# Even attention of a hybrid DiT step: value products in one run per head, score tiles spread a head ahead, TensorE in program order

## The chip, the cores and the metric

The kernel runs on one core of a Trainium2 chip. The time is that of one execution on the device, in microseconds (us). TensorE is called PE in the profile, its weight loads PEld, VectorE is DVE, ScalarE is ACT, GpSimd is POOL and SyncE, which issues the transfers here, is SP.

## The reference

One inference step of a two-layer backbone, for 128 prompt tokens and 512 sample tokens of width 1024. The even layer, on which the change bears, has 8 heads of latent attention (MLA) and 8 query heads on 2 key heads (GQA) side by side; the odd layer (mLSTM and differential attention) is left as it is.

```python
def attend(q, k, v):
    ...
        s = jnp.einsum('bqhgd,bthd->bhgqt', qi, k).astype(jnp.float32) * scale
        p = jax.nn.softmax(s, axis=-1).astype(v.dtype)
        return jnp.einsum('bhgqt,bthd->bqhgd', p, v)
...
    o_a = attend(q_a, k_a, v_a).reshape(B, S, MLA_W) * jax.nn.silu(g_a)
    ...
    o_b = attend(q_bg, kb_all, vb_all).reshape(B, S, GQA_W) * jax.nn.silu(g_b)
    return jnp.concatenate([o_a, o_b], axis=-1) @ w_out, new
```

Each layer is `x + gate * mix(rmsnorm(x) * (1 + scale) + shift)`, where `shift`, `scale` and `gate` are products of a conditioning vector with a weight ("adaptive norm"). Sample queries see 128 cached and 512 own keys, 640 in all; prompt queries see the prompt's 128 keys.

## The kernel before

The even attention (`attention`, L675 to L712, called by `even_attention`, L808 to L833) goes through 16 heads, MLA first. For each head the 512 sample queries are four tiles of 128.

- A **score tile** (`scores`, L596) is 128 queries by 640 keys in two halves of 320: three passes for MLA (the third is the low part `ql` of the queries), two for GQA, into one of two PSUM buffers (`s2`). VectorE takes the negated maximum `nm` (L603), ScalarE the exponential `p` with its sum (L606), VectorE the reciprocal `rs` (L609), GpSimd the normalisation (L616).
- A **transpose group** (`head_T`, L623) turns key tile k of all four query tiles into one PSUM buffer of two (`t1`); ScalarE copies it to `pT` (L628), VectorE for k = 2 (L626).
- The **value products** (`head_PV`, L634) of key tile k are two matmuls side by side, each on 64 columns of the array (`tile_position` (0, 0) and (0, 64)), and add into `o`. With five key tiles a head has ten of these instructions; the trace counts each as two rows. At the head's end `o` is multiplied into the gate buffer `og` (L710).
- `prompt_quad` (L638 to L673) does the prompt's attention for four heads in four stages: queries, scores `sp`, transposes `t1p`, products `op`.
- `side(h)` puts other work into a head: in heads 0 to 7 the odd layer's adaptive columns (`ada_cols`: L177, sixteen rows of 32 columns, a copy `adap` L180, two transposes L184, a reduction and three small VectorE additions, L190 to L195), in heads 8 to 15 the even layer's gate parts (`ada_gate_part`: L210, also 32 columns, copy `gp` L212), the loads of the output projection's weights (`op_load`: `raw`, three buffers shared with the gate's weights; `whi` on ScalarE, L76, `wlo` on GpSimd, L77) and the split of the first half of `og` into `oh` (ScalarE, L841) and `ol` (VectorE, L842). `ada_gate_row` sums the gate's parts (`gsum`, L221), which later go out and come back as a broadcast for the residual.

In the code, key tile k's products are written right after the transposes of key tile k + 1, and score tiles of later heads are written in between by a running count. The code order is only a priority: a scheduler that follows dependences and engine availability sets the order on every engine, TensorE included, and so the order of the sixteen heads' pieces is interleaved. Work on ScalarE, VectorE and GpSimd runs one instruction after another in the order in which it was issued.

Of the kernel before, what the change touches and what calls it, by code (L numbers as in the profile page):

```python
# [37 lines left out]
class K:  # L38
# [3 lines left out]
    # ---------------------------------------------------------------- helpers  # L42
# [8 lines left out]
    def sumsq(self, src, n, w):  # L51
        """sum of squares over groups of w: src [128, n*w] in SBUF -> [128, n]"""
# [14 lines left out]
    def wload(self, src, n, w, pool=None, pre="w", bufs=2, cp=None):  # L67
        """stream a [128, n, w] weight tile and split it into two float32r parts"""
# [18 lines left out]
    def lin_tok(self, pieces, ncols, hh, hl, toks, evac, pool, tag="acc", bufs=5):  # L87
        """out[token, col] for token tiles toks; pieces: [(dram ap, nk)]"""
# [12 lines left out]
    def drain(self, toks, evac, lag=3):  # L101
        """evacuate psum; what evac returns is done lag tiles later"""
# [9 lines left out]
    def lin_feat(self, src, hh, hl, pool, tag="acc", bufs=5):  # L112
        """out[col (128), token (640)] in two psum tiles of 320 tokens"""
# [9 lines left out]
    def silu_from(self, out, src, shape, pool, other=None):  # L123
        """out = silu(src) (times other); src may be PSUM"""
# [8 lines left out]
    def rope(self, out, x, cos, sin, nh, w, pool, rep=1, dup=False):  # L133
        """out = rope(x), [128, nh, w] views; cos, sin [128, w / rep]"""
# [26 lines left out]
    # ---------------------------------------------------------------- adaLN  # L161
# [8 lines left out]
    def ada_cols(self, L, kk, pool, tag, bufs, raws=None, split=False):  # L170
        """shift and gain of feature tile kk as [128, 2] columns (sample, prompt)"""
# [10 lines left out]
        def rest():  # L182
            for i in range(2):
                nc.tensor.transpose(ps[:, 256 + 128 * i:384 + 128 * i], part[:, i * 128:i * 128 + 128], self.ident)  # L184
            red = self.st.tile([128, 2, 2], F32, tag="adar", name="adar", bufs=2)
            nc.vector.tensor_reduce(out=red, in_=ps[:, 256:512].rearrange("p (i g j) -> p i j g", i=2, g=4)[:, :, 0:2],
                                    axis=AX.X, op=ALU.add)
            vg, vs, vc = (V_EG, V_EBS, V_EBC) if L == "e" else (V_OG, V_OBS, V_OBC)
# [11 lines left out]

    def ada_gate_part(self, L, kk, pool, tag, bufs):
        """partial rows of the gate of feature tile kk"""
# [11 lines left out]
    def ada_gate_row(self, L, pool, tag, bufs):  # L214
        """sum of the partial rows of the gate, to DRAM"""
# [12 lines left out]
    def ada_gate_bc(self, L, to):  # L228
        """gate broadcast over partitions: [128, 2, 1024], sample and prompt"""
        self.gate = to  # L230
        for c in range(2):
            self.nc.sync.dma_start(to[:, c], self.gd[L][c:c + 1].to_broadcast([128, 1024]))

    # ---------------------------------------------------------------- body
    def run(self):
        tc, nc, A = self.tc, self.nc, self.A
        with ExitStack() as es:
# [12 lines left out]
            self.GS = {L: (main.tile([128, 8, 2], F32, name="G" + L), main.tile([128, 8, 2], F32, name="S" + L))  # L250
                       for L in "eo"}
# [27 lines left out]
    # ---------------------------------------------------------------- even layer  # L279
    def even(self):  # L280
# [15 lines left out]
        head[0](0, P)  # L296
        head[0](1, P)
# [1339 lines left out]
```

## Time and profile before

| | |
|---|---|
| time, median of 3 runs | 914.14 us (911.05 to 916.01) |
| span of the profiled execution | 905.8 us |
| median less span | 8.3 us |
| TensorE busy | 852.9 us, 94% of the span |
| VectorE, ScalarE, GpSimd busy | 541.2, 422.6, 396.6 us |
| even attention, first score tile to first product of the output projection | 223.0 to 402.1 us |

The profile has no separate time of the profiled execution beside its span; the span counts from its first instruction to its last, and the three timed runs lie 5.3 to 10.2 us above it. Start times are from the start of the span. The busy time of TensorE is modelled from pipelined records, so what one row costs is best read as the step from its start to the next row's start.

### The profile page before, as it was taken

The page shows a single profiled execution, that of the slowest core. Times are in us where ns is not written, and L with a number is a line of the kernel's source. Part 1 is how long each engine was busy: PE and PEld are TensorE (multiplying, and loading weights), DVE is VectorE, ACT ScalarE, POOL GpSimd, SP SyncE. Part 2 cuts the span into 40 slices and gives each one's busy share as a digit, 9 for nine tenths or more (in the row PEclk, how much of TensorE's full clock was granted, in tenths as well). Part 3 has the DMA queues.
Part 4 walks back from the last instruction along what each step waited for, and adds up shares of the span by engine and source line. Part 5 has one row for each costly group of instructions (what it writes and reads, how often), then busy time and mean ns, then how long its engine had stood idle before and what let it go on. Part 6 is the DMA issues. An engine that isn't in the chain of part 4 may idle for free.

```text
span 905.8 us, 14374 instructions
## 1 busy us (share of the span) xinstructions
PE 852.9 (94%) x5418; PEld 707.2 (78%) x5418; DVE 541.2 (60%) x1125; ACT 422.6 (47%) x928; POOL 396.6 (44%) x302
## 2 busy tenths in 40 slices
PE   6999899979999999999999999999999899999997
PEld 2778788879776766668887889889989688778786
DVE  3773831993866877641386735077774736666765
ACT  5354523311655677752263324266554656443422
POOL 0144424751754646725535333422221946354930
PEclk9999999999999999999999999999999999999999
DMA  9821222220221222324412212222123122142503
GB/s 347 330 65 35 88 87 71 70 71 24 94 94 53 84 98 93 119 77 176 152 47 105 86 71 94 81 70 71 47 93 129 58 88 63 55 164 75 163 1 117
DMA packets 29641, 88.52 MB, mean 98 GB/s; under 512 B 3752, under 2 KB 6880, under 8 KB 29572
## 3 DMA queue, kind: packets, MB, share of 16 engines
q1 hardware_dynamic: 25904, 83.64, 26.4%
q10 hardware_dynamic: 3668, 3.96, 1.3%
q8 instruction: 43, 0.70, 0.3%
q14 instruction: 26, 0.21, 0.1%
HBM read 80.90 MB, written 6.68 MB: 97 GB/s over the span
## 4 chain that ended last, share of the span: by engine, by line
PE 74%; DVE 16%; issue 3%; ACT 3%; POOL 2%; DMA 1%; SPq 0%; POOLq 0%; ACTq 0%; DVEq 0%
PE acc L84 11%; PE acc L85 11%; PE acc L83 11%; PE s L596 7%; PE acc L1060 6%; PE o L634 5%; PE t L623 5%; PE acc L120 3%; PE o L1146 2%; PE pv L1460 2%; PE ada L177 1%; POOL wlo L77 1%; DVE nm L603 1%; PE gps L210 1%; PE acc L544 1%
## 5 line engine op out<-in xcount | busy, mean ns | idle before, releaser
L77 POOL TENSOR_TENSOR wlo<-raw,whi 128x1024 fp32r<-128x1024 f32 (+4 forms) x79 | 185.8, 2357 | 229.8 <-ACT whi L76 222.7
L85 PE MATMUL acc<-whi,Hl 128*128 128x512 f32 (+2 forms) x400 | 148.5, 373 | 1.6 <-DVE Hl L958 1.6
L84 PE MATMUL acc<-wlo,Hh 128*128 128x512 f32 (+2 forms) x400 | 149.2, 373 | 0.2 <-POOL wlo L77 0.2
L83 PE MATMUL acc<-whi,Hh 128*128 128x512 f32 (+2 forms) x400 | 138.9, 374 | 1.0 <-ACT qk L1064 1.0
L76 ACT CAST whi<-raw 128x1024 fp32r<-128x1024 f32 (+4 forms) x71 | 71.6, 1010 | 131.2 <-PE acc L85 80.5
L603 DVE TENSOR_REDUCE nm<-s 128x1 f32<-128x640 f32 (+1 forms) x104 | 80.9, 780 | 57.1 <-PE s L596 56.0
L616 POOL TENSOR_TENSOR p<-p,rs 128x640 f32<-128x640 f32 x64 | 79.7, 1256 | 64.2 <-DVE rs L609 62.6
L606 ACT ACTIVATE p<-s,nm 128x640 f32<-128x640 f32 (+1 forms) x104 | 79.4, 764 | 59.8 <-DVE nm L603 53.9
L85 PEld LDWEIGHTS acc<-whi,Hl 128*128 128x128 f32 x400 | 75.3, 188 | 14.7 <-DVE Hl L958 1.8
L83 PEld LDWEIGHTS acc<-whi,Hh 128*128 128x128 f32 x400 | 75.1, 188 | 14.0 <-ACT qk L1064 1.2
L84 PEld LDWEIGHTS acc<-wlo,Hh 128*128 128x128 f32 x400 | 75.4, 188 | 12.9 <-POOL wlo L77 0.6
L48 POOL TENSOR_TENSOR rs_r<-rs_h,mhalf 128x1 f32<-128x1 f32 (+4 forms) x39 | 35.6, 921 | 53.4 <-DVE rs_h L47 45.0
L623 PEld LDWEIGHTS t<-cst,p 128*128 128x128 f32 x320 | 34.6, 140 | 23.6 <-issue 22.1
L623 PE MATMUL t<-cst,p 128*128 128x128 f32 x320 | 51.3, 283 | 0.2 <-POOL p L616 0.2
L84 PE MATMUL acc<-wlo,oh 128*128 128x512 f32 (+1 forms) x124 | 48.1, 388 | 0.1
L85 PE MATMUL acc<-whi,ol 128*128 128x512 f32 (+1 forms) x124 | 47.8, 386 | 0.0
L83 PE MATMUL acc<-whi,oh 128*128 128x512 f32 (+1 forms) x124 | 46.7, 389 | 0.0
L628 ACT COPY pT<-t 128x512 f32<-128x512 f32 x64 | 37.1, 584 | 17.4 <-PE t L623 17.0
L120 PE MATMUL acc<-Hh,whi 128*128 128x320 f32 x128 | 31.3, 316 | 6.9 <-DVE og L129 6.9
L63 DVE TENSOR_REDUCE ssq<-sq 128x2 f32<-128x128 f32 (+3 forms) x19 | 11.5, 604 | 40.6 <-ACT sq L61 40.4
L885 ACT ACTIVATE junk<-xt 128x512 bf16<-128x512 f32 (+1 forms) x21 | 12.8, 610 | 49.0 <-DVE xt L883 37.7
L1060 PE MATMUL acc<-Hh,whi 128*128 128x320 f32 x128 | 32.5, 323 | 0.5 <-ACT v L1037 0.5
(380 smaller groups left out, 1983.2 us busy)
## 6 DMA issues: line engine op xcount, KB each, us to landing
adaw<-in_eada_ss_dram SPq DMA_DIRECT2D x16, 512.0 KB, 10.3
raw<-in_oada_ss_dram SPq DMA_DIRECT2D x16, 512.0 KB, 4.3
raw<-in_e_wG_dram SPq DMA_DIRECT2D x8, 512.0 KB, 3.3
raw<-in_eada_g_dram SPq DMA_DIRECT2D x8, 512.0 KB
raw<-in_e_wO_dram SPq DMA_DIRECT2D x8, 512.0 KB, 4.2
raw<-in_oada_g_dram SPq DMA_DIRECT2D x8, 512.0 KB, 3.5
raw<-in_o_wO_dram SPq DMA_DIRECT2D x8, 512.0 KB, 3.9
xT<-in_xT_dram SPq DMA_DIRECT2D x8, 320.0 KB, 5.8
```

What stands on the lines that cost most here:

```text
L76: (cp or nc.scalar.copy)(hi[:, 0:m], raw[:, 0:m])
L77: nc.gpsimd.tensor_tensor(out=lo[:, 0:m], in0=raw[:, 0:m], in1=hi[:, 0:m], op=ALU.subtract)
L83: mm(out, lhsT=lh, rhs=rh, start=first, stop=False)
L84: mm(out, lhsT=lh, rhs=rl, start=False, stop=False)
L85: self.mark = mm(out, lhsT=ll, rhs=rh, start=False, stop=last)
L120: mm(acc[j][:, 0:320], lhsT=a[:, k], rhs=b[:, k, j * 320:j * 320 + 320], start=f, stop=l)
L596: self.mark = self.nc.tensor.matmul(out[:, j, 0:w], lhsT=q[0:rows, qcols], rhs=k[0:rows, a:a + w], start=i == 0, stop=i == len(passes) - 1)
L603: nc.vector.tensor_reduce(out=nm, in_=s, axis=AX.XY, op=ALU.max, negate=True)
L606: nc.scalar.activation(out=p[:, 0:n].rearrange("p (a b) -> p a b", a=s.shape[1]), in_=s, func=AF.Exp, bias=nm, accum_out=sm)
L616: self.nc.gpsimd.tensor_tensor(out=p, in0=p, in1=rs.to_broadcast([128, 640]), op=ALU.mult)
L623: self.nc.tensor.transpose(tp[:, i * 128:i * 128 + 128], p[i][:, k * 128:k * 128 + 128], self.ident)
L1060: nc.tensor.matmul(acc[j][:, 0:320], lhsT=a[:, k], rhs=b[:, k, j * 320:j * 320 + 320], start=f, stop=l)
```

## The change

1. The ten value products of a head are written after its fifth transpose group, in one run; `o` is allocated there. The `pT` buffers go from 3 to 7, the `p` buffers from 10 to 8.
2. Score tiles are written one after each transpose group: tiles 1, 2 and 3 of the next head after groups 0, 1 and 2, and tile 0 of the head after that behind group 4. Prompt stages go behind group 3, or 4 for the last stage.
3. A context `pe_order` ties each TensorE instruction of the attention to the one before it in the code, so that TensorE runs in the order in which the program is written. It adds no semaphore wait. The other engines stay with the scheduler.
4. `side(h)` comes behind the products: one feature tile of adaptive columns per head 0 to 7, whose two transposes and reduction come a score tile later in the next head; the additions of shift and gain are done once for all eight tiles (`ada_close`). One gate part per head 8 to 15; the gate's sum follows the last products.
5. `prep` is split in `keys` (the cast and low part `Ka` of a head's keys) and `queries` (transposes and split), each at its own place.
6. The split of the first half of `og` takes its low part on GpSimd; that of the second half stays on VectorE.

```diff
+    @contextmanager
+    def pe_order(self):
...
+        for a, b in zip(pe, pe[1:]):
+            self.tc.add_manual_dep(b, a.name, mybir.DependencyInfo(mybir.DependencyClass.NoSync,
+                                                                   mybir.DependencyReason.DATA), reason="pe_order")
...
-        p, rs = self.softexp(T, s, 640, 10)
+        p, rs = self.softexp(T, s, 640, 8)
...
-        pT = T.tile([128, 512], F32, tag='pT', name='pT', bufs=3)
+        pT = T.tile([128, 512], F32, tag='pT', name='pT', bufs=7)
...
         for h in range(nh):
-            o = ps.tile([128, 512], F32, tag='o', name='o', bufs=1)
-            pt = {}
             p = [tiles.pop((h, i)) for i in range(4)]
-            for k in range(6):
-                if k < 5:
-                    pt[k] = self.head_T(T, ps, p, k)
-                if k:
-                    self.head_PV(o, V[h], cols[h], pt.pop(k - 1), k - 1)
-                if k == 0 and h + 2 < nh:
-                    prep(h + 2, P)
-                if k == 2:
-                    side(h)
-                if k in (3, 5):
-                    next(stages, None)
-                more_scores(4 * h + 5 + 1 + min(k, 3) + (1 if k >= 4 else 0))
+            pt = [self.head_T(T, ps, p, 0)]
+            if h + 2 < nh:
+                prep[0](h + 2, P)
+            scores(h + 1, 1)
+            if rest:
+                rest()
+            pt.append(self.head_T(T, ps, p, 1))
+            scores(h + 1, 2)
+            if h + 2 < nh:
+                prep[1](h + 2, P)
+            pt.append(self.head_T(T, ps, p, 2))
+            scores(h + 1, 3)
+            pt.append(self.head_T(T, ps, p, 3))
+            done = stage(0, 1, 2)
+            pt.append(self.head_T(T, ps, p, 4))
+            scores(h + 2, 0)
+            if not done:
+                stage(3)
+            o = ps.tile([128, 512], F32, tag='o', name='o', bufs=1)
+            for k in range(5):
+                self.head_PV(o, V[h], cols[h], pt[k], k)
...
+            rest = side(h)
...
-                for i in ((0, 1), (2,), (3,), (4,), (5,), (), (6,), (7,))[h]:
-                    self.ada_cols('o', i, ps, 'pr', 1)
+                rest = self.ada_cols('o', h, ps, 'pr', 1, split=True)
+                return rest if h < 7 else lambda: (rest(), self.ada_close())
...
-            for i in ((0,), (1,), (2,), (3,), (), (4,), (5, 6), (7,))[h - 8]:
-                self.ada_gate_part('e', i, ps, 'pr', 1)
+            self.ada_gate_part('e', h - 8, ps, 'pr', 1)
...
-        self.nc.vector.tensor_tensor(out=lo, in0=src, in1=hi, op=ALU.subtract)
+        (self.nc.vector if m else self.nc.gpsimd).tensor_tensor(out=lo, in0=src, in1=hi, op=ALU.subtract)
```

TensorE in an MLA head, before; `t` are transpose groups, `o` value products (one row of x2 is one key tile), `s` score tiles, `ada` the transposes of adaptive columns, `qtp` queries:

```order
L634 MATMUL o<-pT,Va 64x256 x2
L184 MATMUL ada<-cst,adap 128x128 x2
L634 MATMUL o<-pT,Va 64x256 x2
L623 MATMUL t_2550<-cst,p 128x128 x4
L634 MATMUL o<-pT,Va 64x256 x2
L623 MATMUL t_2587<-cst,p 128x128 x4
L777 MATMUL qtp<-cst,qa 128x128 x4
L634 MATMUL o<-pT,Va 64x256 x2
L623 MATMUL t_2639<-cst,p 128x128 x4
L634 MATMUL o<-pT,Va 64x256 x2
L623 MATMUL t_2657<-cst,p 128x128 x4
```

The same engine in an MLA head after the change, from the third transpose group on:

```order
L621 MATMUL s_3061<-Ka_1592,qh 128x320 x2
L621 MATMUL s_3061<-Ka_1591,ql 128x320 x2
L648 MATMUL t_3076<-cst,p 128x128 x4
L685 MATMUL t1p<-cst,pp 128x128 x4
L648 MATMUL t_3090<-cst,p 128x128 x4
L621 MATMUL s_3097<-Ka_1593,qh 128x320 x2
L621 MATMUL s_3097<-Ka_1594,qh 128x320 x2
L621 MATMUL s_3097<-Ka_1593,ql 128x320 x2
L659 MATMUL o<-pT,Va 64x256 x10
L190 MATMUL ada<-raw,sc 32x256 x8
L648 MATMUL t_3140<-cst,p 128x128 x4
```

The products stand in one run of ten behind the fifth group and a score tile, with the 32-column products of the adaptive norm right behind them.

GpSimd around the move from MLA to GQA heads, before; `p` are normalisations of score tiles, `pp` those of the prompt, `wlo` the low part of a piece of output weights:

```order
L656 TENSOR_TENSOR pp<-pp,sm_2953 128x512
L616 TENSOR_TENSOR p<-p,rs 128x640 x7
L656 TENSOR_TENSOR pp<-pp,sm_3254 128x512
L616 TENSOR_TENSOR p<-p,rs 128x640 x11
L77 TENSOR_TENSOR wlo<-raw,whi 128x1024
L616 TENSOR_TENSOR p<-p,rs 128x640 x7
L77 TENSOR_TENSOR wlo<-raw,whi 128x1024
```

And after:

```order
L641 TENSOR_TENSOR p<-p,rs 128x640 x13
L884 TENSOR_TENSOR ol_3679<-og,oh_3678 128x512
L884 TENSOR_TENSOR ol_3812<-og,oh_3811 128x512
L884 TENSOR_TENSOR ol_3936<-og,oh_3935 128x512
L884 TENSOR_TENSOR ol_4088<-og,oh_4087 128x512
L884 TENSOR_TENSOR ol_4217<-og,oh_4216 128x512
L641 TENSOR_TENSOR p<-p,rs 128x640 x3
L681 TENSOR_TENSOR pp<-pp,sm_3503 128x512
L641 TENSOR_TENSOR p<-p,rs 128x640 x10
L77 TENSOR_TENSOR wlo<-raw,whi 128x1024
```

The five low parts of the split stand in one row among the normalisations; before, they were on VectorE.

ScalarE in a GQA head in which output weights are loaded, before:

```order
L606 ACTIVATE p,sm<-s_3848,nm 128x640
L628 COPY pT<-t_3801 128x512
L76 CAST whi<-raw 128x1024
L212 COPY gp<-gps 128x128
L606 ACTIVATE p,sm<-s_3870,nm 128x640
L606 ACTIVATE p,sm<-s_3892,nm 128x640
L628 COPY pT<-t_3861 128x512
L628 COPY pT<-t_3883 128x512
```

And after:

```order
L653 COPY pT<-t_3815 128x512
L653 COPY pT<-t_3835 128x512
L631 ACTIVATE p,sm<-s_3822,nm 128x640
L76 CAST whi<-raw 128x1024
L631 ACTIVATE p,sm<-s_3842,nm 128x640
L653 COPY pT<-t_3875 128x512
L844 CAST qp<-qtp 64x2x128
L631 ACTIVATE p,sm<-s_3862,nm 128x640
L653 COPY pT<-t_3890 128x512
L631 ACTIVATE p,sm<-s_3897,nm 128x640
```

In both, the cast `whi` of the loaded weights stands among the exponentials `p,sm` and the copies `pT`; after, it stands between the exponentials of the next head's second and third score tiles.

## Rows read from the trace of the kernel before

**Rows 1.** The page: busy time of each engine, its share of the span, and instructions.

```profile
PE 852.9 (94%) x5418; PEld 707.2 (78%) x5418; DVE 541.2 (60%) x1125; ACT 422.6 (47%) x928; POOL 396.6 (44%) x302
```

**Rows 2.** Busy time by window, of the attention stretch: start and end, length, then busy time and instructions of PE, PEld, DVE, ACT, POOL, the granted clock of TensorE, the busy share of the transfers and GB/s.

```profile
223.00:402.10 179.10, 173.36 (x1382) 118.52 (x1381) 124.34 (x260) 116.65 (x272) 103.61 (x80) 1.00 0.26 90
```

**Rows 3.** Waits of PE in the same stretch, the three longest sums: engine and line, what it waited for, us in total, times, longest.

```profile
PE o L634 <- DVE rs L609: 1.6, 1, 1.6
PE s L596 <- ACT p L606: 1.1, 4, 0.4
PE t1p L660 <- POOL pp L656: 1.0, 1, 1.0
```

**Rows 4.** Timeline of PE in head 13 and 14: start, busy us, line, operation, and how many instructions of a kind stand in a row.

```profile
388.43 0.66 PE L623 MATMUL t<-cst,p 128*128 128x128 f32 x4
388.84 0.82 PE L596 MATMUL s<-Kb,q 128*128 128x320 f32 x4
389.60 0.65 PE L634 MATMUL o<-pT,Vb 128*64 128x256 f32 x4
390.18 0.66 PE L623 MATMUL t<-cst,p 128*128 128x128 f32 x4
390.76 0.65 PE L634 MATMUL o<-pT,Vb 128*64 128x256 f32 x4
391.35 1.09 PE L623 MATMUL t<-cst,p 128*128 128x128 f32 x8
392.38 1.08 PE L634 MATMUL o<-pT,Vb 128*64 128x256 f32 x8
393.39 0.66 PE L623 MATMUL t<-cst,p 128*128 128x128 f32 x4
```

**Rows 5.** Timeline of PE: the first and the last of the 76 runs of value products in the stretch.

```profile
239.99 0.65 PE L634 MATMUL o<-pT,Va 128*64 128x256 f32 x4
...
400.70 1.45 PE L634 MATMUL o<-pT,Vb 128*64 128x256 f32 x8
```

**Rows 6.** Groups by line and shape in the stretch: count, busy us in all and mean ns of one, then the idle time ahead of them and who ended it.

```profile
L616 POOL TENSOR_TENSOR p<-p,rs 128x640 f32<-128x640 f32 x64 | 79.7, 1256 | 64.2 <-DVE rs L609 62.6 <-PE t L623 1.0 <-PE o L634 0.4
L603 DVE TENSOR_REDUCE nm<-s 128x1 f32<-128x640 f32 x64 | 52.4, 820 | 24.2 <-PE s L596 23.5
...
L606 ACT ACTIVATE p<-s,nm 128x640 f32<-128x640 f32 x64 | 51.0, 797 | 33.2 <-DVE nm L603 27.7 <-DVE rs L609 3.0 <-DVE adar L186 1.2
L628 ACT COPY pT<-t 128x512 f32<-128x512 f32 x64 | 37.1, 584 | 17.4 <-PE t L623 17.0
...
L710 DVE TENSOR_TENSOR og<-o,og 64x256 f32<-64x256 f32 x30 | 12.5, 418 | 5.4 <-PE o L634 5.0
L606 ACT ACTIVATION_READ_ACCUMULATOR p<-s,nm 128x1 f32 x64 | 12.5, 195 | 0.0
...
L77 POOL TENSOR_TENSOR wlo<-raw,whi 128x1024 fp32r<-128x1024 f32 x4 | 9.5, 2364 | 3.7 <-ACT whi L76 3.7
L761 POOL TENSOR_TENSOR Ka<-kn,Ka 64x640 fp32r<-64x640 f32 x6 | 9.3, 1549 | 6.9 <-DVE Ka L760 4.6 <-PE t L623 1.8 <-DVE rs L609 0.5
L177 PE MATMUL ada<-raw,sc 128*32 128x256 f32 x128 | 8.6, 385 | 0.1
...
L210 PE MATMUL gps<-raw,sc 128*32 128x128 f32 x128 | 5.5, 279 | 0.0
...
L76 ACT CAST whi<-raw 128x1024 fp32r<-128x1024 f32 x4 | 4.2, 1048 | 1.2 <-DMA raw<-in_e_wO_dram 1.2
...
L841 ACT CAST oh<-og 128x512 fp32r<-128x512 f32 x6 | 3.4, 626 | 0.0
```

**Rows 7.** Timeline of POOL at the start of the stretch; the normalisations are those of the third and fourth score tile of head 0.

```profile
232.12 1.29 POOL L616 TENSOR_TENSOR p<-p,rs 128x640 f32<-128x640 f32 x1
233.38 0.72 POOL L783 TENSOR_TENSOR kp<-kn,kp 64x256 fp32r<-64x256 f32 x1
234.07 1.30 POOL L616 TENSOR_TENSOR p<-p,rs 128x640 f32<-128x640 f32 x1
```

**Rows 8.** Timeline of PE at the start of the stretch: one score tile and what follows it.

```profile
224.99 0.85 PE L596 MATMUL s<-Ka,qh 96*128 96x320 f32 x4 [0.97 <-DVE og L129]
225.67 0.46 PE L596 MATMUL s<-Ka,ql 96*128 96x320 f32 x2
225.97 0.60 PE L777 MATMUL qtp<-cst,qa 128*128 128x128 f32 x4
```

**Rows 9.** One line of the kernel on POOL (a low part of 128 x 512, elsewhere in the kernel): min, median and max ns, first and last start.

```profile
L958 POOL TENSOR_TENSOR Hl<-h,Hh x5: 1310/1312/2725, 457.7 to 475.9; 128x512 fp32r<-128x512 f32 x5
```

**Rows 10.** The transfers into the `raw` buffers from 330 to 402 us: time from issue to landing.

```profile
DMA to landing us min/median/max: 3.4/4.2/5.0
```

**Rows 11.** Timeline of DVE in head 8: two low parts of the split, one after the other.

```profile
340.41 3.45 DVE L842 TENSOR_TENSOR ol<-og,oh 128x512 fp32r<-128x512 f32 x2
```

**Rows 12.** Busy time by window, at two gaps of PE outside the stretch; columns as in rows 2, the granted clock is the third column from the end.

```profile
98.70:101.10 2.40, 0.00 (x0) 0.00 (x0) 2.40 (x4) 0.37 (x1) 1.95 (x2) 1.00 0.24 53
101.10:104.50 3.40, 3.09 (x11) 3.12 (x12) 2.99 (x16) 1.02 (x3) 0.70 (x1) 0.50 0.83 305
718.00:721.00 3.00, 0.23 (x2) 0.23 (x3) 2.92 (x3) 0.23 (x2) 3.00 (x2) 1.00 0.05 5
721.00:724.00 3.00, 3.00 (x17) 2.57 (x17) 1.93 (x4) 2.63 (x9) 3.00 (x4) 1.00 0.46 169
```

More of the change, by code (lines that the diff above doesn't have):

```diff
@@ L1 @@
 import math
-from contextlib import ExitStack
+from contextlib import ExitStack, contextmanager
 import numpy as np
@@ L159, in rope @@
         nc.vector.tensor_tensor(out=out, in0=v1, in1=v2, op=ALU.add)
+    @contextmanager
+    def pe_order(self):
+        ins = lambda: self.nc.cur_bb.bb.instructions
+        first = ins()[-1]
+        yield
+        now = list(ins())
+        at = next(k for k in reversed(range(len(now))) if now[k] is first) + 1
+        pe = [i for i in now[at:] if i.engine == self.mark.ins.engine]
+        for a, b in zip(pe, pe[1:]):
+            self.tc.add_manual_dep(b, a.name, mybir.DependencyInfo(mybir.DependencyClass.NoSync,
+                                                                   mybir.DependencyReason.DATA), reason="pe_order")
     def ada_load(self, L, kk, to=None):
@@ L295, in even @@
         P = {}
-        head[0](0, P)
-        head[0](1, P)
+        for h in range(2):
+            for f in head[0]:
+                f(h, P)
         self.even_gates(H, L2, ps)
@@ L678, in attention, with scores, stage @@
         tiles = {}
-        state = {"s": 0}
-        def more_scores(upto):
-            while state["s"] < min(upto, 4 * nh):
-                h, i = divmod(state["s"], 4)
+        stages = [(q, i) for q in quads for i in range(4)]
+        def scores(h, i):
+            if h < nh:
                 tiles[h, i] = self.head_scores(T, ps, P[h], i)
-                state["s"] += 1
-        stages = (x for q in quads for x in q)
-        more_scores(4)
-        next(stages, None)
-        next(stages, None)
-        for h in range(nh):
-            o = ps.tile([128, 512], F32, tag="o", name="o", bufs=1)
-            pt = {}
-            p = [tiles.pop((h, i)) for i in range(4)]
-            for k in range(6):
-                if k < 5:
-                    pt[k] = self.head_T(T, ps, p, k)
-                if k:
-                    self.head_PV(o, V[h], cols[h], pt.pop(k - 1), k - 1)
-                if k == 0 and h + 2 < nh:
-                    prep(h + 2, P)
-                if k == 2:
-                    side(h)
-                if k in (3, 5):
-                    next(stages, None)
-                more_scores(4 * h + 5 + 1 + min(k, 3) + (1 if k >= 4 else 0))
+        def stage(*kinds):
+            if stages and stages[0][1] in kinds:
+                next(stages.pop(0)[0])
+                return True
+        for i in range(4):
+            scores(0, i)
+        stage(0)
+        scores(1, 0)
+        rest = None
+        for h in range(nh):
+            p = [tiles.pop((h, i)) for i in range(4)]
+            pt = [self.head_T(T, ps, p, 0)]
[16 more added lines that the diff above has]
+                stage(3)
+            o = ps.tile([128, 512], F32, tag="o", name="o", bufs=1)
+            for k in range(5):
+                self.head_PV(o, V[h], cols[h], pt[k], k)
             r = slice(64 * (h % 2), 64 * (h % 2) + 64)
@@ L740, in even_prep, with keys, queries @@
                                       krT[i][:, None, 640:768].to_broadcast([32, 2, 128]))
-        def prep(h, P):
+        def keys(h, P):
+            if h >= 8:
+                return
+            e = h % 2
+            kh, kl = Ka[e]
+            src = kn[NR[e], h // 2, 0:640]
+            nc.vector.tensor_copy(kh[NR[e]], src)
+            nc.gpsimd.tensor_tensor(out=kl[NR[e]], in0=src, in1=kh[NR[e]], op=ALU.subtract)
+        def queries(h, P):
+            if h >= 8 and h % 2:
+                return
             tp = self.prep_ps()
             if h >= 8:
-                if h % 2:
-                    return
                 m, g = (h - 8) // 2, (h - 8) // 4
@@ L830, in side @@
                 self.op_split(self.R, 0, h - 9)
-        self.attention(T, ps, P, prep, [Va] * 8 + [Vb] * 8, [64 * h for h in range(8)] + [64 * (h // 4) for h in range(8)],
-                       side, quads)
+        with self.pe_order():
+            self.attention(T, ps, P, prep, [Va] * 8 + [Vb] * 8, [64 * h for h in range(8)] + [64 * (h // 4) for h in range(8)],
+                           side, quads)
     def op_split(self, P, m, t):
```

31 lines of the change are left out of this document (18 added, 13 removed).

## The prediction

> **What bounds the kernel now.** I read the busy line of the page first [rows 1]: TensorE is busy for 852.9 us, 94% of the span, and no other engine passes 60%. So this change can pay only through TensorE, in the stretch that it touches: the even layer's attention, from the first score tile at 223.0 to the first product of the output projection at 402.1. The windows view [rows 2] says what holds that stretch: TensorE 173.4 busy of 179.1 us at full clock, VectorE 124, ScalarE 117, GpSimd 104. The waits view [rows 3] puts names to nearly all of the 5.7 us of idle time; the longest came once. The reader should see two things here. There are about 5.7 us of waiting to win at most; the rest must come out of the busy time. And VectorE, ScalarE and GpSimd have slack over the whole stretch, which says nothing yet about one head.
>
> Inside the busy time, the timeline of one late head [rows 4] shows a cost that no duration column names. Four transposes ahead of products take 0.58 us from start to start, eight take 1.03: four more cost 0.45, so the run of four holds 0.13 that belongs to no transpose. Four value products take 0.59, eight 1.01: 0.42 for four, so 0.17 belongs to none. The transposes use the whole array and the products a 64-column tiling of it, so each change between the two costs about (0.13 + 0.17) / 2 = 0.15 us.
>
> **The change, part by part.**
>
> *Value products in one run.* Before, the products fall into 76 runs, from 239.99 to 400.70 [rows 5]; with the 32-column products of the adaptive norm and the gate, the timeline has 181 changes of tiling in the stretch. After, by program order, each head has three (into the products, on to the 32-column products, back): about 47. 134 x 0.15 = 20.1 us leave TensorE's own time: 173.4 - 20.1 = 153.3. A direct step from 64 to 32 columns after products is not in the trace in this place; if it costs nothing, 16 x 0.15 = 2.4 us more are gained, and if it costs as much as two changes, 2.4 us fewer; I count it as one.
>
> What covered the cost so far is the scheduler's freedom: it filled TensorE's waits with whatever was ready. That freedom goes with the fixed order, so I set all 5.7 us of old waits to zero and charge the new ones head by head.
>
> *The start.* Head 0's first transposes need all four of its tiles normalised on GpSimd. Before, the third started at 232.12, a prompt copy came at 233.38 and the fourth at 234.07 [rows 7]; that copy is now later, so the fourth ends near 232.12 + 1.29 + 1.30 = 234.7 and the group near 234.9, 11.9 us after 223.0. In order, TensorE has before that point five score tiles at 0.98, one queries group at 0.60 and the four transposes at 0.41 [rows 4, 8]: 5.9 us. Wait: **6.0 us**, where the old order put prompt scores and adaptive columns in. With the copy left where it was it is 6.7; if the norms tighten, 4.
>
> *MLA heads (0 to 7).* From a finished score tile to its normalised one: 0.82 on VectorE, 0.80 and 0.20 on ScalarE, 1.26 on GpSimd [rows 6], with some 0.6 allowed for the reciprocal and the steps between engines: 3.7 us. Between the last tile of a head that is scored late, and the transposes that want it, stand two transpose groups, a score tile, the products (0.17 + 20 x 0.105 = 2.3) and the adaptive columns (8.6 / 8, some 1.0): 5.5. So **0**; the key parts on GpSimd (1.55, [rows 6]) may push in ahead of a norm, which bounds it at 4 us for all eight.
>
> *GQA heads (8 to 15), two score buffers.* The tile two places later needs the buffer that an exponential still reads: 0.82 + 0.80 and some 0.4 of steps, 2.0 after the tile's end, against 0.41 + 0.76 + 0.41 = 1.6 of work in between [rows 4, 6]. I take 0.5 in heads without a queries group and 0.1 with one: **2.4 us**, bounds 0 and 5.
>
> *Split of the first half's output, moved to GpSimd.* Five subtractions now stand in one row on GpSimd ahead of three norms of head 9. The nearest row is a subtraction of that shape there: 1.31 median [rows 9]; the bounds are 1.18, half of a low part twice as wide (2.36, [rows 6]), and 2.73, its longest. After head 7's products: 0.84 for two gate products, 0.63 cast [rows 6], 5 x 1.31, 3 x 1.26 = 11.8. Head 9's transposes are due at some 10.4: a GQA head is five transpose groups (2.3), four score tiles (3.0), products (2.3) and gate products (5.5 / 8 = 0.7), 8.3 [rows 4, 6], and head 8 has some 2 more of prompt scores and queries. **1.5 us**, bounds 0 and 8. On the other side the old wait of 1.6 [rows 3] goes for good: there VectorE held two of these subtractions for 3.45 us beside a GpSimd subtraction [rows 11]. The Trainium skill's "SBUF — State Buffer" (section on who interferes with whom) says that a VectorE operation with two SBUF inputs and a GpSimd one lock each other out whole; the trace agrees, and by that rule the moved subtractions meet nothing, since the reductions beside them read PSUM.
>
> *Weights of the output projection (heads 11 to 14).* Three raw buffers serve the gate's weights and these. A load starts when the previous head's gate products have freed one and lands 3.4 to 5.0 us later [rows 10]; ScalarE's cast of it (1.05) stands between two exponentials, and GpSimd's low part (2.36, [rows 6]) between two norms. Before, TensorE took other work meanwhile. Landing 4.4 to 5.0, cast 1.05, low part 2.36, two norms 2.5: 10.3 to 10.9 us into a head. Its own work is 8.3, and the next head's first group, which needs these norms, is due some 0.3 later: 1.7 to 2.3 late. At 1.9 a head, **7.7 us** over four heads, bounds 0 (if two norms slip ahead of the low part) and 10.
>
> *The tail.* Head 15 has no scores to put between its groups; two transpose buffers wait for copies of 0.58 [rows 6], three groups some 0.3 late each: **1.0**. The gate row's sum, moved behind the last products, waits for a ScalarE copy: **0.6**. The tiny additions per feature tile that fall away, and the split of key and query work, are VectorE work beside a TensorE that does not wait for them: 0.
>
> *Sum.* 6.0 + 0 + 2.4 + 1.5 + 7.7 + 1.0 + 0.6 = 19.2 us of waits, on 153.3 of work: 172.5 against 179.1, 6.6 us less. The profiled execution's span is 905.8, 8.3 below the median of 914.14; I carry that difference along: 914.1 - 6.6 = **907.5 us**.
>
> **The clock.** After 2.4 us and more without a product at 98.7, the granted clock stood at 0.50, which is 1.2 GHz, from 101.1 to 104.5; after 718 a gap as long left it at 1.00 [rows 12]. The start now has such gaps. A half-speed stretch of that length costs 1.7 us. The Trainium skill's "TensorE: Matmul & The Clock Gate" (Part 1) holds that an idle TensorE is throttled, which speaks against an order with a long wait in it; by it the time would be 909.2. The rows go both ways, so I leave it out of the sum and in the range.
>
> **The rivals.** (a) *Waits stay cheap.* The other engines catch up before TensorE asks, because a head still takes 8 to 10 us. Then 6 to 14 us of waits remain, for the start above all, and the time is 894 to 902. For it: 104 to 124 busy of 179 [rows 2]. Against it: within a GQA head, GpSimd's norms and low part are 4 x 1.26 + 2.36 = 7.4 us [rows 6], nearly the head. (b) *The gain is eaten.* Waits of 24 to 30 us give 912 to 918: every bound above taken halfway up. (c) *Slower.* One mechanism: the loads themselves. A buffer of the output weights comes free only when GpSimd has made the low part, some 8 us into a head; the gate weights of a later head queue behind it, and TensorE, which can no longer pass over the gate products, waits for the landing too. 3 to 4 us more in each of four heads, 12 to 16, gives 35 us of waits at the most and 31 at the least: 919 to 923. It decides once the waits pass 20.1 + 5.7 = 25.8 us. For it: three buffers, two loads a head. Against it: the gate products of before had no idle time ahead of them [rows 6]. (d) *It does not do what it says*: the order shows the products in runs of ten instructions, so only the price per change can fail; at half of it, 10 us less gain, the time is 917.5, with (b).
>
> **How the numbers follow.** Forecast, waits of 14 to 24 us, 902 to 912: 0.45. (a) 0.25, (b) with (d) 0.17, (c) 0.13. Half a per cent is 4.6 us, about what a measurement tells from no change: faster is below 909.6, slower above 918.7. Faster: all of (a) and four fifths of the forecast, 0.61. Same: the rest of the forecast and (b), 0.26 with (d). Slower: 0.13. The range leaves out (c) and the lowest part of (a): 896.5 to 918.5.
>
> **What would show it.** Right: no more than some 50 changes of tiling, a product run of 2.3 us per head, TensorE busy near 153 in the stretch, a wait near 6 us before the first transposes, and waits in heads 11 to 14 put down to GpSimd's norms or ScalarE's casts. Wrong: runs of products much longer than 2.3 us; new waits in the MLA heads, where I put none; gate products that wait for a landing; or the clock at 0.50 after the start.

## The result: slower by one per cent, and the profile after

The changed kernel takes 921.87 us (median of 15 runs, 915.86 to 925.83), the kernel before 911.05 (15 runs, 908.68 to 917.65). The ratio is 1.0101, 95% interval 1.0073 to 1.0129: **slower by 9 to 11 us**, where 6.6 us less was forecast. The profiled execution spans 920.5 us.

The page shows where to look: TensorE's busy time is the same as in [rows 1], and the row of granted clock, 23 us to a digit, is no longer all nines.

```profile
PE 852.4 (93%) x5418; PEld 725.8 (79%) x5418; DVE 528.4 (57%) x1099; ACT 423.3 (46%) x928; POOL 402.8 (44%) x307
...
PEclk9999999999799999999998999999999899999999
```

The window of the attention and, under it, its start, columns as in [rows 2]:

```profile
224.30:408.20 183.90, 164.14 (x1383) 130.68 (x1381) 114.61 (x241) 119.16 (x276) 109.88 (x85) 0.95 0.24 81
228.85:242.50 13.65, 11.55 (x46) 10.28 (x45) 5.74 (x12) 5.88 (x14) 8.47 (x7) 0.50 0.00 1
242.50:256.00 13.50, 13.42 (x115) 11.22 (x113) 10.17 (x21) 9.43 (x26) 9.06 (x9) 1.00 0.23 78
```

The stretch is 183.9 us long, not 179.1. TensorE is busy for 164.1 of it (forecast 153.3) and idle for 19.8 (forecast 19.2). In the 13.65 us from 228.85 to 242.5 the granted clock is 0.50, which is 1.2 GHz; in [rows 2] it is 1.00 throughout. Another 3.4 us at 0.50 follow at 372: 17.1 us at half speed in the stretch, none before.

The waits of TensorE there, as in [rows 3], longest sums first:

```profile
PE sp L672 <- ACT p L631: 4.0, 2, 2.2
PE s L621 <- ACT p L631: 3.9, 8, 0.6
PE t L648 <- POOL p L641: 2.4, 3, 1.3
PE t L648 <- ACT pT L653: 2.3, 5, 1.2
PE acc L83 <- DVE grow L248: 1.4, 1, 1.4
PE gsum L245 <- ACT gp L236: 1.3, 1, 1.3
PE ada L197 <- ACT adap L193: 1.0, 1, 1.0
PE op L693 <- ACT pT L653: 1.0, 1, 1.0
```

And the end of the stretch on TensorE:

```profile
401.79 2.38 PE L659 MATMUL o<-pT,Vb 128*64 128x256 f32 x20
404.10 0.64 PE L234 MATMUL gps<-raw,sc 128*32 128x128 f32 x16
406.08 0.64 PE L245 MATMUL gsum<-gp,cst 128*32 128x256 f32 x8 [1.34 <-ACT gp L236]
408.14 0.50 PE L83 MATMUL acc<-whi,oh 128*128 128x512 f32 x1 [1.42 <-DVE grow L248]
```

The twenty rows of products take 401.79 to 404.10, 2.31 us: the run that the change is about costs what was forecast. Behind it the gate's sum waits for a ScalarE copy and the output projection for the row made of it, 1.34 and 1.42 us.

### The profile page after: what moved, and what is told of

Read it like the earlier page. It is cut to its first block, busy times and chain, and to the rows that moved or that the text cites. A ratio compares the mean times of both kernels' runs of the same rounds, so it can differ in the third digit from the quotient of the medians.

```text
span 920.5 us, 14387 instructions
## 1 busy us (share of the span) xinstructions
PE 852.4 (93%) x5418; PEld 725.8 (79%) x5418; DVE 528.4 (57%) x1099; ACT 423.3 (46%) x928; POOL 402.8 (44%) x307
## 4 chain that ended last, share of the span: by engine, by line
PE 71%; DVE 15%; ACT 5%; issue 4%; POOL 3%; DMA 2%; SPq 0%; POOLq 0%; ACTq 0%; DVEq 0%
PE acc L84 11%; PE acc L85 11%; PE acc L83 11%; PE s L621 7%; PE acc L1102 6%; PE o L659 3%; PE acc L120 3%; PE t L648 3%; PE pv L1502 2%; PE o L1188 2%; ACT p L631 1%; PE ada L190 1%; POOL wlo L77 1%; DMA adaw<-in_eada_ss_dram 1%; DVE nm L628 1%
## 5 line engine op out<-in xcount | busy, mean ns | idle before, releaser
L77 POOL TENSOR_TENSOR wlo<-raw,whi 128x1024 fp32r<-128x1024 f32 (+4 forms) x79 | 186.0, 2360 | 235.2 <-ACT whi L76 228.1
L84 PE MATMUL acc<-wlo,Hh 128*128 128x512 f32 (+2 forms) x400 | 151.2, 378 | 0.2 <-POOL wlo L77 0.2
L648 PEld LDWEIGHTS t<-cst,p 128*128 128x128 f32 x320 | 38.2, 144 | 12.7 <-POOL p L641 4.5
L120 PE MATMUL acc<-Hh,whi 128*128 128x320 f32 x128 | 31.3, 316 | 6.9 <-DVE og L129 6.9
L634 DVE RECIPROCAL rs<-sm 128x1 f32<-128x1 f32 x104 | 16.5, 160 | 30.5 <-ACT p L631 29.3
```

Source lines behind the costliest of these rows:

```text
L77: nc.gpsimd.tensor_tensor(out=lo[:, 0:m], in0=raw[:, 0:m], in1=hi[:, 0:m], op=ALU.subtract)
L84: mm(out, lhsT=lh, rhs=rl, start=False, stop=False)
L120: mm(acc[j][:, 0:320], lhsT=a[:, k], rhs=b[:, k, j * 320:j * 320 + 320], start=f, stop=l)
L648: self.nc.tensor.transpose(tp[:, i * 128:i * 128 + 128], p[i][:, k * 128:k * 128 + 128], self.ident)
```

## Experiments

Two readings ran against each other. (A): waits of the fixed order, at the start above all, and the half-speed clock that follows them. (B): the clock falls anywhere by chance. Later readings joined: (C), waits of the fixed order in the later heads, and (D), which gives their cause: long pieces on ScalarE and GpSimd, whose order is free behind a fixed order on TensorE.

### The kernel before again, and a second profile of the changed one

No edit. Each run lists the mean granted clock of its core.

> The kernel before, once more, for its clock from run to run. The theory (A): the changed kernel loses at the start of the attention, where TensorE in fixed order waits for the first normalised tiles and its clock stands at 0.5 for 13.7 us; then the kernel before should show a mean clock near 0.995 in most runs and no half-speed stretch between 223 and 245. The rival (B): half-speed stretches come by chance anywhere; then the mean clock of the kernel before should spread over some 0.975 to 0.995 from run to run, and those in the changed kernel say little. Time near 911 us by both.

909.99 us (12 runs), mean clock 0.982 to 0.993, no half-speed time between 223 and 402, but 18 us of it behind.

> The changed kernel once more, for a second profile. So far at equal mean clock all kernels lie within some 3 us, and the changed one differs by its half-speed time: 46 us a run on average against 21. (A) The half-speed time is made in the attention by its waits: again some 10 us or more of it between 224 and 408, by the start and by the waits of the prompt scores near 329 and 370. (B) It lies anywhere: the stretch shows little and the rest of the kernel more than 20 us.

928.70 us, one run; 17.9 us at half speed in the stretch (234, 333, 374 and at its end), 25.2 behind it, of which 6.0 are the rest of the one at its end.

The stretch itself is 177.5 us long in the second profile of the kernel before (179.1 in the first) and 187.9 in that of the changed one (183.9). The two first profiles differ by 14.7 us of span, 4.8 of them in the stretch; outside it the changed kernel's has some 35 us at half speed and the other's 11. The two second ones differ by 14.8 us, 10.4 of them in the stretch; outside it, half-speed time is near equal, 35 and 32 us.

Here the clock's price can be read. Over 12 runs of the kernel before, the span rises by 0.89 us for each 0.001 that the mean clock falls; over 15 of the changed kernel by 0.85. A clock lower by 0.001 is some 1.84 us more at half speed (0.002 of 920), so a microsecond at half speed costs 0.46 to 0.48 us. (Four further sets of runs of the kernel before give slopes of 0.65 to 1.00, so 0.35 to 0.54 us.) Half-speed time is (1 - mean clock) / 0.5 x span: 45.7 us a run for the changed kernel, 20.6 for the one before. The 25.1 us more are worth some 12 us, 9 to 14 by the wider range. Read off both lines at a mean clock of 0.985, the spans are 912.1 for the kernel before and 911.3 for the changed one, whose own runs reach only 0.980: at equal clock no difference can be told, and the 6.6 us of the forecast are not there either. (B) is half right: half-speed time comes and goes outside the stretch by run (4.6 to 25.2 us behind it in these profiles). But inside, it is there in both profiles of the changed kernel and in neither of the other.

### The start, free or kept busy

```diff
+        order = self.pe_order()
         for h in range(nh):
+            if h == 1:
+                order.__enter__()
...
+        order.__exit__(None, None, None)
...
-        with self.pe_order():
+        if True:
```

> The changed kernel, but TensorE's order is fixed only from head 1 on; head 0 is left to the scheduler. (A) The start is filled as in the kernel before, the half-speed stretch there goes, and some 7 us of clock and 3 us of waiting come back: 911 to 914 us, ratio 1.000 to 1.003. (B) The start is not what costs: 919 to 923 us, ratio 1.008 to 1.012. A third reading (C), waits of the fixed order in the later heads, expects the same as (B), and the waits of heads 6 to 15 unchanged at some 12 us.

914.12 us (12 runs), ratio 1.0057 (1.0032 to 1.0082): 4 us of the 9 come back. The start runs at full clock; half-speed stretches now stand at 327.5 and 368.5, behind the waits of the prompt scores in heads 8 and 12 (1.8 and 2.8 us). Between (A) and (B).

```diff
         for i in range(4):
             scores(0, i)
+            keep((8, 4, 0, 0)[i])
         stage(0)
         scores(1, 0)
+        keep(30)
```

`keep(n)` writes n transposes of a constant into a buffer that nothing reads.

> The changed kernel with 42 more transposes of a constant into a PSUM buffer that nothing reads: 8 and 4 after the first two score tiles of head 0 and 30 ahead of its first transpose group. They add 4.6 us of TensorE work where it waits anyway. (A) If TensorE's waiting is what halves the clock there, the stretch between 229 and 242 runs at 1.0 and some 5 to 7 us come back although nothing waits less: 914 to 917 us, ratio 1.003 to 1.006. (B) and (C): no gain or up to 2 us lost, 920 to 924 us.

920.77 us (6 runs), 1.0107 (1.0073 to 1.0141). The clock did what (A) said:

```profile
222.80:243.00 20.20, 18.83 (x143) 17.23 (x144) 13.11 (x27) 11.22 (x25) 11.41 (x9) 1.00 0.00 1
```

Full speed through the start, and head 0 ends 22.0 us after the first score tile in place of 25.0. The time did not follow. The stretch is 183.4 us long, against 183.9 and 187.9 in the two profiles of the changed kernel: in head 8 TensorE waited 3.0 us for the prompt scores (1.8 and 3.0 in those two), and the clock fell to 0.50 there for 6.8 us. The start was not the whole; against the first of those profiles, head 8 took back what came early.

### Without the fixed order

```diff
-        with self.pe_order():
+        if True:
```

> The changed kernel without the fixed order: products in one run per head, tiles and side work as written, everything else left to the scheduler. (A) 905 to 912 us: the start is filled, and few of the 20 us of changes of tiling come back, since the products are still written in one run. (C) Also the waits of the later heads go: 895 to 903 us, ratio 0.98 to 0.99. If the scheduler splits the runs of products again, more than 100 changes of tiling return and the time is that of the kernel before, 909 to 913 us.

908.62 us (12 runs), 1.0001 (0.9979 to 1.0023): the last line of the expectation. The scheduler split the products into 72 runs, 169 changes of tiling. Hardly a wait is left, and no half-speed time:

```profile
223.10:399.50 176.40, 173.44 (x1382) 120.16 (x1380) 111.89 (x234) 114.63 (x272) 109.48 (x85) 1.00 0.28 91
```

The 20 us of changes saved and the waits that the order brought stand against each other here: 173.4 busy and 3 idle, against 164.1 busy (at half speed for a part) and 20 idle.

### Four places

Prompt scores went behind the fifth transpose group, the late score tile behind the fourth, prompt products behind the value products, and the gate row into head 15, for which two of the gate's parts came one head earlier. The first of these by itself, with the order fixed from the start:

```diff
-            done = stage(0, 1, 2)
+            done = stage(0, 2)
             pt.append(self.head_T(T, ps, p, 4))
+            if not done:
+                done = stage(1)
             scores(h + 2, 0)
```

> The changed kernel with the prompt scores one transpose group later, behind the fifth group, where the score buffer they want is free; the order stays fixed everywhere. (A) The two waits of 2.1 to 2.4 us go, some 4 us of waiting, and with them the half-speed stretches at 329 or 370; the start still falls: 915 to 918 us, ratio 1.004 to 1.007. If only the waiting counts and not the clock: 4 us, 917 to 918. If another wait takes their place, the next score tile's: no change, 1.010.

924.81 us (6 runs), 1.0146 (1.0112 to 1.0181): no gain, and above the changed kernel by an amount at the edge of the intervals. The prompt scores waited 1.2 us in place of 4.0, but a transpose group now waited 2.7 us for a VectorE copy in head 8: another wait took its place, though not the one that the last line of the expectation names.

All four, with head 0 free:

> Head 0 left to the scheduler, order fixed from head 1 on, and four waits taken away by place alone: prompt scores behind the fifth group, the third late score tile behind the fourth group in place of the third, prompt products behind the value products, the gate row in head 15 instead of behind it. (A) Waits of the stretch fall from some 17 to under 7 us, no half-speed stretch is left in it: 896 to 902 us, ratio 0.985 to 0.993. If waits only move: 908 to 914. If TensorE's clock still falls in the stretch: 902 to 908.

909.35 us (12 runs), 0.9984 (0.9958 to 1.0009): no difference from the kernel before. 14.6 us of idle time are left in the stretch, and 6.8 at half speed.

> The same four moves, but the order fixed from the start, head 0 included. It parts the start from the rest. (A) The start alone costs some 3 us of waiting and up to 7 us of clock: 5 to 10 us above the run with head 0 free, 902 to 911 us, and a half-speed stretch between 229 and 243. (C), the later heads were all of it: within 2 us of that run.

917.88 us (12 runs), 1.0079 (1.0045 to 1.0112), above either reading's range; 13.7 us at half speed from 228.4. The fixed start alone costs 8.6 us here ((1.0079 - 0.9984) x 910), 4 in the pair above.

The longest wait left in the run at 0.9984 stood in head 8 (one of 2.5 us for a GpSimd norm follows at 390). On VectorE, GpSimd and TensorE:

```profile
318.75 1.29 DVE L221 TENSOR_TENSOR gso<-gso,cols 128x16 f32<-128x16 f32 x1
319.96 1.31 DVE L222 TENSOR_TENSOR gso<-gso,cols 128x16 f32<-128x16 f32 x1
321.31 1.19 DVE L223 SCALAR_TENSOR_TENSOR gso<-gso,cols 128x16 f32<-128x16 f32 x1
```

```profile
316.25 6.22 POOL L891 TENSOR_TENSOR ol<-og,oh 128x512 fp32r<-128x512 f32 x5
```

```profile
320.51 0.82 PE L621 MATMUL s<-Kb,q 128*128 128x320 f32 x4
323.94 1.11 PE L648 MATMUL t<-cst,p 128*128 128x128 f32 x4 [2.60 <-DVE pT L651]
```

Three additions over 16 columns take 1.2 to 1.3 us each beside the five GpSimd subtractions of the split, a VectorE copy comes late, and TensorE stands still for 2.60 us.

### The price of a change

```diff
             pt.append(self.head_T(T, ps, p, 1))
+            self.head_PV(o, V[h], cols[h], pt[0], 0)
...
-            for k in range(5):
-                self.head_PV(o, V[h], cols[h], pt[k], k)
+            self.head_PV(o, V[h], cols[h], pt[4], 4)
```

> The run with four moves and head 0 free, but the value products of a key tile stand behind the next tile's transposes, as before the change; TensorE's order stays fixed. It puts the 0.15 us per change to the test: some 120 changes come back, 18 us of TensorE work. If the price is right and waits stay as they are, 18 us more, 925 to 929 us. If waits are set by ScalarE and GpSimd, the changes fill them: 5 to 10 us more, 914 to 920 us, with fewer waits and less half-speed time. If a change costs nothing in truth, no more.

925.45 us (6 runs), 1.0169 (1.0142 to 1.0196). Of this run and of the one at 0.9984, from which it differs in this alone:

```profile
223.20:415.80 192.60, 177.87 (x1382) 121.62 (x1381) 111.96 (x234) 117.30 (x272) 109.61 (x85) 0.98 0.24 83
```

```profile
223.70:398.50 174.80, 160.18 (x1382) 126.98 (x1380) 113.51 (x234) 116.13 (x272) 109.55 (x85) 0.98 0.26 87
```

177.9 against 160.2 busy, 174 against 56 changes of tiling, 6.8 us at half speed in both: 17.7 / 118 = 0.150 us a change. The price stood. The waits did not swallow it: idle time was 14.7 us, and 14.6 without the changes.

### Work tied to its place on ScalarE and GpSimd

First the three additions alone, written behind head 15 in the code:

```diff
+            if h == 15:
+                self.ada_close()
```

> The run with four moves and head 0 free, with one more move: the three VectorE additions over all eight feature tiles, which stood in head 8, come behind head 15. In head 8 they took 1.2 to 1.3 us each beside the five GpSimd subtractions, and TensorE waited 2.6 us behind them. (A) That wait and the half-speed stretch of 6.8 us near 324 go: 4 to 6 us less than that run, 903 to 906 us, ratio 0.991 to 0.995. If GpSimd's five subtractions hold the norms anyway: the wait turns into one for a norm, and less than 2 us are gained. If clock falls do not hang on such waits, 2 to 3 us.

910.81 us (12 runs), 1.0013 (0.9990 to 1.0035). It tested nothing: the scheduler of VectorE pulled the additions back to 319, between the same rows. Where a piece stands in the code does not place it on an engine whose order is free.

Then ties like those of TensorE's order, without a semaphore wait: a cast behind the exponential that the program wrote last (`emark`), a low part behind the norm written last (`pmark`).

```diff
+        a = self.nc.scalar.copy(hi, src)
+        b = (self.nc.vector if m else self.nc.gpsimd).tensor_tensor(out=lo, in0=src, in1=hi, op=ALU.subtract)
+        if not m:
+            self.tie(a, self.emark)
+            self.tie(b, self.pmark)
```

> The run at 894 us without the ties of the output weights' parts: only the split of the first half is tied. (D) The row of five subtractions in head 8 costs most, through the additions and the norms behind it: 899 to 903 us, ratio 0.990 to 0.994, with the waits of 1.6, 1.6 and 2.8 us in heads 11 to 15 as before the ties. If the weights' parts cost as much by themselves: 904 to 908 us.

903.19 us (6 runs), 0.9907 (0.9872 to 0.9942). The split tied, one a head, is worth 9.6 us ((1.0013 - 0.9907) x 910); the two intervals lie apart. The next run ties the output weights' cast and low part as well and, which its expectation does not say, issues their loads one head earlier (heads 11 to 14 in place of 12 to 15).

> As the last, and the split of the first half (ScalarE and GpSimd) and the output weights' parts tied to places: one split a head behind the exponential and the norm issued last, the weights' parts likewise, so that neither five subtractions stand in a row nor a cast that waits for its load stands between two exponentials. (A) Another 5 to 7 us of waits in heads 9 to 15 go (1.6 twice, 2.7 once): 896 to 901 us, ratio 0.984 to 0.990. (C) If GQA heads are bound by ScalarE and GpSimd themselves, the waits only move: no gain, within 2 us of the last.

893.95 us (6 runs, four at 893 to 894 and two at 902), **0.9853 (0.9815 to 0.9892)**: the median lies below what was expected, the ratio inside it. This run beats both kernels by 13 us and more. Against the one before it is 4.9 us, with intervals that overlap, and the ties of the weights are not parted from their earlier loads. The same additions, now with no subtraction beside them, and the waits and the window that are left:

```profile
317.73 0.17 DVE L229 TENSOR_TENSOR gso<-gso,cols 128x16 f32<-128x16 f32 x1
317.82 0.17 DVE L230 TENSOR_TENSOR gso<-gso,cols 128x16 f32<-128x16 f32 x1
318.77 0.16 DVE L231 SCALAR_TENSOR_TENSOR gso<-gso,cols 128x16 f32<-128x16 f32 x1
```

```profile
PE s L629 <- ACT p L639: 3.2, 4, 1.4
PE s L629 <- DVE og L132: 1.0, 1, 1.0
PE gps L242 <- ACT gp L244: 0.6, 1, 0.6
PE sp L680 <- ACT p L639: 0.6, 1, 0.6
```

```profile
223.30:388.90 165.60, 159.26 (x1382) 126.15 (x1380) 110.09 (x234) 115.94 (x272) 109.56 (x85) 0.98 0.27 90
```

> The run at 894 us with TensorE's order fixed from the start, head 0 included: the start alone. (A) 6 to 10 us more, 900 to 904 us, ratio 0.990 to 0.995, a half-speed stretch between 228 and 243 and 10 us or more of half-speed time above that run. If the start's price fell on waits that are gone now: within 2 us of it.

901.62 us (6 runs), 0.9889 (0.9859 to 0.9919). By the ratios the fixed start costs 3.3 us, by the medians 7.7; with six runs each the intervals overlap, so its price is not shown by this pair. The clock is: 10.2 us at half speed from 228.1, where the run with head 0 free has none.

> The changed kernel with one edit: the split of the first half and the output weights' parts are tied to places on ScalarE and GpSimd, one a head, as in the run at 894 us; TensorE's order is fixed from the start, prompt scores and gate row stand where the change put them. If the free placement on ScalarE and GpSimd is the main cost of the change (D): 905 to 909 us, ratio 0.995 to 1.000, at most one wait over 2 us left in heads 8 to 15. If the start and the four places are (A): 914 to 919 us, ratio 1.005 to 1.010.

908.88 us (12 runs), 0.9982 (0.9960 to 1.0003). The ties, on the changed kernel with its order and places as they are, take back 10.8 us ((1.0101 - 0.9982) x 910), the loads one head earlier included: (D) had it. Half-speed time falls with it, from 45.7 to 35.7 us a run, worth some 5 of the 10.8 us. Its stretch, and the waits of 1 us and more:

```profile
224.80:398.80 174.00, 160.16 (x1382) 127.44 (x1381) 111.72 (x241) 119.29 (x276) 110.05 (x85) 0.98 0.26 86
```

```profile
PE s L629 <- ACT p L639: 4.5, 9, 0.7
PE t L656 <- POOL p L649: 2.8, 2, 1.9
PE acc L86 <- DVE grow L256: 1.4, 1, 1.4
PE t L656 <- ACT pT L661: 1.4, 5, 0.3
PE gsum L253 <- ACT gp L244: 1.3, 1, 1.3
PE s L629 <- DVE og L132: 1.0, 1, 1.0
```

Compared with the changed kernel, 9.9 us of the stretch are gone: 3.9 busy and 6 idle. No wait above 1.5 us stands outside the start, and no half-speed time either: 6.8 us are left in place of 17.1, all of them in the start.

## Why the prediction was wrong

**Changes of tiling: right.** 48 were counted where 47 were forecast, a run of products costs 2.31 us, and 0.150 us a change was measured by itself.

**The sum of the waits: near, by luck.** 19.2 us were forecast, 19.8 measured (23.7 in the second profile), but the terms differ. The start was put at 6.0; its waits are 3.6 (1.0, 0.5 and 2.1), probably because TensorE at half speed came later to what it waited for. The score buffers were put at 2.4: 3.4. The output weights, the largest term, were put at 7.7 us, four heads late by GpSimd's norms; the longest wait for a norm behind them is 0.3 us, and behind ScalarE's casts there are 2.2 us in head 12, 1.2 in head 13 and 1.0 in head 14. The tail was put at 1.6: 0.9 in head 15 and 2.8 for the gate row make 3.7. The prompt scores in GQA heads, 4.0 us (head 12's 2.2 among them), were not in the sum at all: they too want one of the two score buffers.

In the two places where they waited, the pieces behind it were the split and the output weights, as forecast, but the waits came about in another way. In head 8, of the changed kernel, VectorE, GpSimd, ScalarE and TensorE:

```profile
326.73 1.32 DVE L221 TENSOR_TENSOR gso<-gso,cols 128x16 f32<-128x16 f32 x1
327.98 0.16 DVE L222 TENSOR_TENSOR gso<-gso,cols 128x16 f32<-128x16 f32 x1
328.17 1.14 DVE L223 SCALAR_TENSOR_TENSOR gso<-gso,cols 128x16 f32<-128x16 f32 x1
329.31 0.80 DVE L628 TENSOR_REDUCE nm<-s 128x1 f32<-128x640 f32 x1
```

```profile
324.27 6.22 POOL L884 TENSOR_TENSOR ol<-og,oh 128x512 fp32r<-128x512 f32 x5
```

```profile
330.20 0.79 ACT L631 ACTIVATE p<-s,nm 128x640 f32<-128x640 f32 x1 [1.72 <-DVE nm L628]
```

```profile
331.14 1.11 PE L672 MATMUL sp<-Kb,qp 128*128 128x128 f32 x8 [1.81 <-ACT p L631]
```

Five subtractions in one row of 6.22 us, as forecast, 1.24 each; what was not forecast is that two of the three new additions take 1.1 to 1.3 us beside them, 0.17 without. The maximum of a score tile comes only behind the additions, the exponential behind the maximum, and the prompt scores behind the exponential, whose score buffer they want. The prediction had written that the moved subtractions "meet nothing". The Trainium skill's "SBUF — State Buffer" (section on who interferes with whom) was used too narrowly there: I looked only at the reductions, and the additions of `ada_close` have two SBUF inputs. By the rule they wait for a GpSimd operation to end, and the rows agree: the third and the fourth subtraction end at 328.02 and 329.28, the first and the third addition at 328.05 and 329.31.

In head 12, ScalarE and TensorE:

```profile
369.59 1.04 ACT L76 CAST whi<-raw 128x1024 fp32r<-128x1024 f32 x1 [1.14 <-DMA raw<-in_e_wO_dram]
...
371.02 0.79 ACT L631 ACTIVATE p<-s,nm 128x640 f32<-128x640 f32 x1
```

```profile
369.19 0.60 PE L648 MATMUL t<-cst,p 128*128 128x128 f32 x4
371.95 0.91 PE L672 MATMUL sp<-Kb,qp 128*128 128x128 f32 x4 [2.16 <-ACT p L631]
```

The cast of the output weights waits for its load with an exponential behind it, and TensorE with both: 2.16 us. A wait of that size was priced, at 1.9 a head, but for norms behind GpSimd's low part, and in four heads.

**TensorE's own time: wrong, and with it the forecast.** 153.3 us were forecast, 164.1 measured: 10.8 of the 11.4 us by which the stretch is longer than forecast. The step that failed is the one on the clock: "The rows go both ways, so I leave it out of the sum and in the range", at 1.7 us. There were 17.1 us at half speed in the stretch, not one of 3.4, worth some 8 us by the line above (6 to 9 by the wider range). The error was to treat the clock as one possible event at the start. The forecast itself put 19 us of waits into a stretch that had 5.7 before, so the new waits should have carried a share of half-speed time, and with it the 20 us gained were not enough. Some 3 us of the busy time stay unexplained: with 6.8 us at half speed it is 159.3 and 160.2 in the tied runs, more than 153.3 + 3.3, and 2 us of it are there at full clock too, in the run without the fixed order (173.4 us with 12 changes fewer than before).

The profile from which the forecast was made showed the clock smaller than it is. Its mean clock of 0.995 is above that of all 12 runs of the same kernel. Of the 8.3 us between its span and the median time, which the prediction carried along, only 1.8 lie between the span and the time of one and the same run (1.7 to 1.9 in the changed kernel's 15); the rest is the spread from run to run.

Was it the clock or the waits? The runs say that the two come together, without a fixed rule. In the six profiles in which head 0 runs in fixed order, the clock falls between 228 and 237; in the ten in which it is free, kept busy or as before, it stays at 1.00 up to 245. So the start's fall is not chance. In the later heads falls stand behind waits of some 1 to 3.4 us, but the 1.8 us in head 8 of the changed kernel's first profile and two of 1.4 us in the run at 901.62 brought none. Taking away 6 us of idle time with the ties took 9.9 us off the stretch; keeping TensorE busy at the start kept the clock at 1.00 and brought head 0 to its end 3 us sooner. How much of the 25 us of half-speed time per run is due to the stretch is only shown for two profiles (17.1 and 17.9). Outside, it differs from run to run too much to divide.

**The rivals.** (b) and (c) together were nearest, (c) by its price, 919 to 923, not by its mechanism: its 31 us of waits were 19.8, and the gate products never waited for a landing. **"What covered the cost so far is the scheduler's freedom"** was right, and went one engine too short: once TensorE's order is fixed, the freedom left on ScalarE, VectorE and GpSimd works against it, since it puts five subtractions or a cast that waits ahead of what TensorE needs next.

## What to carry to other kernels

Fixing the order of the engine that bounds a kernel is half a step: long pieces on the engines that feed it need places too, or they stand in front of the short ones that it waits for. Taken together with a free first head and four places, that made 20 us of saved tiling changes worth 13 us, after they had been worth less than nothing. When waits are traded for work on TensorE, price a microsecond of waiting above one: in the one pair of profiles compared here, a microsecond of waiting taken away in the stretch gave 1.6 (9.9 / 6).

## What the runs showed that I had not expected

- A change of tiling costs 0.150 us, the same from a timeline of four rows and from 118 changes put back.
- The same gap does or does not bring the clock down. Behind the attention, TensorE waits 2.9 us from 717.9 in the profile of before without a fall, and 2.9 us from 728.5, after the same work, in that of the changed kernel with 6.8 us at 0.50. So one profile's mean clock says little about a kernel: 12 runs of the kernel before spread from 0.982 to 0.993 and 10 us with it.
- An addition over 16 columns on VectorE took 0.17 us alone and 1.29 beside a GpSimd subtraction, with whose end it ended.
